# Seven block products for the FFN's first product, the FFN in parts of 8, 8 and 6 tiles, and conditioning vectors in PSUM

## The chip, the cores and the metric

One core of one Trainium2 chip runs the kernel. The metric is the device time of one execution in microseconds; a lower one is better.

## What is computed

One step of a small diffusion backbone of two layers, for 512 latent tokens and 128 context tokens that share the weights. Each layer: a modulated RMSNorm, a projection into three attention branches, their merge, an output projection, a second modulated norm and a SwiGLU FFN. The part that matters here:

```python
def swiglu(h, w_ffn_in, w_ffn_out):
    a, b = jnp.split(h @ w_ffn_in, 2, axis=-1)
    return (jax.nn.silu(a) * b) @ w_ffn_out

def modulation(cvec, w_mod, b_mod):
    m = jax.nn.silu(cvec) @ w_mod + b_mod
    return [t[:, None, :] for t in jnp.split(m, N_MOD, axis=-1)]
...
    x = x + g2 * swiglu(rmsnorm(x, lp['norm2_g']) * (1.0 + sc2) + sh2, lp['w_ffn_in'], lp['w_ffn_out'])
```

The width is 1024, the FFN's inner width 2816, that is 22 tiles of 128; `modulation` is computed for two vectors, that of the request and that of the context. All is float32.

## The kernel before

**Data.** Activations lie transposed: 8 k-tiles of 128 features by 640 tokens, taken in two halves of 320. A float32 product runs as three TensorE passes over split operands: `group` (lines 404 to 414) multiplies high by high, high weight by low input and low weight by high input. Each weight chunk (128 x 1024) is loaded to `raw`, its high part copied by ACT to `whi` (line 311) and its low part, `raw - whi`, made by POOL into `wlo` (line 350). There are two `raw` buffers and four each of `whi` and `wlo`; `weights` (line 357) runs this for all chunks in the order of `plan`.

**FFN.** `ffn_in` takes a part of the inner tiles. A tile has a gate chunk and a value chunk; for each half of the tokens it makes both products over 8 k-tiles into one PSUM tile `S`, then `after` applies silu (ACT, to `s`), multiplies by the value (DVE, `s<-s,S`), and splits the result into high (ACT) and low (DVE, `act<-s,act`). `ffn_out` then multiplies the part's tiles with the second weight and adds the result to the residual `x` (DVE, `x<-S,mo,x`). There were two parts of 11 tiles (`SEG`). `FO_SPLIT` says from which step of the last part the first half of the tokens is finished before the second, so that the norm of the first half can begin.

**Conditioning.** `mod_dve` computes modulation on DVE while other work runs: 512 columns of the transposed weight come to `mr`, and a multiply with a running sum over silu of the vector, `cb` in SBUF (line 515), gives one partial sum. There are 24 sets a layer; 8 are made at the kernel's start in other ways, 12 behind the first attention, the rest in layer 0's FFN.

**Order.** A planner (`_Order`) writes out the order of every engine from estimated costs when the program is built; `DVE`, `ACT`, `POOL` and `SP` then go strictly in that order. Each generator has a priority (lower first: norms 8, weight preparation 20, work behind a product 40, conditioning 200, the dense products 1000), and conditioning fills what is left. Its cost in the plan is `MOD_SPREAD`. `SP` issues all loads.

Of the kernel before, what the change touches and what calls it, by code (L numbers as in the profile page):

```python
# [32 lines left out]
P = 128  # L33
# [37 lines left out]
WO_SPLIT, FO_SPLIT = 4, 66  # L71

SEG = 11
PARTS = [range(a, min(a + SEG, NF)) for a in range(0, NF, SEG)]

# [7 lines left out]
MOD_SOON, MOD_SPREAD = 0.7, 1.4  # L83
# [172 lines left out]
class _Trunk:  # L256
# [41 lines left out]

    def ev(self):
        return _Event()  # L300
# [56 lines left out]
    def weights(self, plan):  # L357

        self.chunks = []
        todo = []  # L360
        for p in plan:
            c = {"src": p, "loaded": self.ev(), "hi_ok": self.ev(), "lo_ok": self.ev()}
            todo.append(c)
        self.chunks = list(todo)

        def load(c):
            c["raw"] = yield from self.get("raw", [P, CH])
            yield self.dma(c["raw"], self.I["w"][c["src"]], 128 * 4 * CH)
            self.o.fire(c["loaded"])

        def hi():
            for c in todo:
                yield self.wait(c["loaded"])
                yield ("acq", "whi")
                yield ("acq", "wlo")
                c["hi"], c["lo"] = self.t("whi", [P, CH], F32R), self.t("wlo", [P, CH], F32R)
                yield self.act(c["hi"], c["raw"], AF.Copy)
                self.o.fire(c["hi_ok"])

        def lo():  # L380
            for c in todo:
                yield self.wait(c["hi_ok"])
                yield self.ptt(c["lo"], c["raw"], c["hi"].bitcast(F32), ALU.subtract)
                self.rel("raw")
                self.o.fire(c["lo_ok"])
# [6 lines left out]
        for g in (load_rest, hi, lo):  # L392
            self.o.spawn(g(), 20)
        return [lambda c=c: load(c) for c in todo[:2]]

    def chunk(self):
        c = self.chunks.pop(0)
        yield self.wait(c["lo_ok"])
        return c["hi"], c["lo"]
# [89 lines left out]
    def mod_dve(self, sets, prio, each):  # L489
# [3 lines left out]
        pieces = [(l, j, q, i, self.ev(), {}) for l, j in sets for q in range(2) for i in range(2)]  # L493

        def load():
            cb = yield from self.get("cb", [P, 2, D])
            yield self.dma(cb, self.I["cb"], 128 * 8 * D)
            yield self.act(cb, cb, AF.Silu)
            self.cb = cb
            self.o.fire(cb_ok)  # L500
            for l, j, q, i, e, d in pieces:
                d["raw"] = yield from self.get("mr", [P, 512])
# [1488 lines left out]
```

## Time and profile before

| | us |
|---|---|
| three runs, median (lowest to highest) | 2482.03 (2476.64 to 2484.36) |
| profiled execution, its own time | 2480.7 |
| its span, first to last instruction | 2478.9 |
| PE busy in the span | 2381.0 |
| DVE, ACT, POOL busy | 1646.1, 1097.4, 907.2 |
| mean granted clock of PE | 0.983 of 2.4 GHz |

A busy share is an average over the whole span. A row of a timeline gives the start in us from the span's beginning, the duration, the engine, the line and the operation, with its output and inputs by the program's tile names; square brackets tell how long the engine had been idle and what ended that.

### The profile page before, as it was taken

The page shows a single profiled execution, that of the slowest core. Times are in us where ns is not written, and L with a number is a line of the kernel's source. Part 1 is how long each engine was busy: PE and PEld are TensorE (multiplying, and loading weights), DVE is VectorE, ACT ScalarE, POOL GpSimd, SP SyncE. Part 2 cuts the span into 40 slices and gives each one's busy share as a digit, 9 for nine tenths or more (in the row PEclk, how much of TensorE's full clock was granted, in tenths as well). Part 3 has the DMA queues.
Part 4 walks back from the last instruction along what each step waited for, and adds up shares of the span by engine and source line. Part 5 has one row for each costly group of instructions (what it writes and reads, how often), then busy time and mean ns, then how long its engine had stood idle before and what let it go on. Part 6 is the DMA issues. An engine that isn't in the chain of part 4 may idle for free.

```text
span 2478.9 us, 44317 instructions
## 1 busy us (share of the span) xinstructions
PE 2381.0 (96%) x17084; PEld 2332.7 (94%) x17084; DVE 1646.1 (66%) x3924; ACT 1097.4 (44%) x2566; POOL 907.2 (37%) x656
## 2 busy tenths in 40 slices
PE   7998889999999999999989998999999999999997
PEld 4998889999988999999989997999999999999997
DVE  7588898678799666676677879887774462212224
ACT  5666566556323322122257664666552342212221
POOL 3534322433433433333345434224333343333331
PEclk9999999999999999999999999999999999999999
DMA  6211111111454444344422111101112322222221
GB/s 235 88 45 57 38 43 35 48 52 44 145 191 141 153 143 150 133 156 139 150 88 70 53 59 43 35 29 63 44 52 73 106 77 77 77 77 71 75 77 60
DMA packets 84739, 216.54 MB, mean 87 GB/s; under 512 B 9648, under 2 KB 23600, under 8 KB 84272
## 3 DMA queue, kind: packets, MB, share of 16 engines
q1 hardware_dynamic: 84528, 213.71, 25.6%
q8 instruction: 135, 2.21, 0.4%
q14 instruction: 76, 0.62, 0.1%
HBM read 206.85 MB, written 6.82 MB: 86 GB/s over the span
## 4 chain that ended last, share of the span: by engine, by line
PE 76%; DVE 18%; issue 2%; ACT 1%; DMA 1%; POOL 0%; SPq 0%; DVEq 0%; ACTq 0%
PE S L411 12%; PE S L410 12%; PE S L412 12%; PE B L410 6%; PE B L412 6%; PE B L411 6%; PE B L1024 3%; PE B L718 3%; PE B L720 3%; PE B L719 3%; PE S L996 2%; PE S L995 2%; DVE nu L338 2%; DVE P L346 2%; PE B L1260 2%
## 5 line engine op out<-in xcount | busy, mean ns | idle before, releaser
L350 POOL TENSOR_TENSOR wlo<-raw,whi 128x1024 fp32r<-128x1024 f32 x268 | 659.6, 2465 | 906.6 <-ACT whi L311 906.2
L411 PE MATMUL S<-h,whi 128*128 128x320 f32 x1408 | 438.7, 312 | 6.5 <-DVE h L338 5.8
L410 PE MATMUL S<-h,whi 128*128 128x320 f32 x1408 | 438.5, 311 | 0.0
L412 PE MATMUL S<-h,wlo 128*128 128x320 f32 x1408 | 437.4, 311 | 0.0
L311 ACT ACTIVATE whi<-raw 128x1024 fp32r<-128x1024 f32 x268 | 282.8, 1056 | 271.7 <-PE S L411 227.2
L718 PE MATMUL B<-whi,h 128*128 128x256 f32 x928 | 278.3, 300 | 1.0 <-DVE u L334 0.5
L411 PEld LDWEIGHTS S<-h,whi 128*128 128x128 f32 x1408 | 266.1, 189 | 9.4 <-DVE h L338 7.0
L720 PE MATMUL B<-whi,h 128*128 128x256 f32 x928 | 266.3, 287 | 3.7 <-DVE h L338 3.1
L410 PEld LDWEIGHTS S<-h,whi 128*128 128x128 f32 x1408 | 266.1, 189 | 0.8 <-ACT h L311 0.4
L412 PEld LDWEIGHTS S<-h,wlo 128*128 128x128 f32 x1408 | 266.3, 189 | 0.0
L719 PE MATMUL B<-wlo,h 128*128 128x256 f32 x928 | 265.7, 286 | 0.0
L515 DVE SCALAR_TENSOR_TENSOR md<-mr,cb 128x512 f32<-128x512 f32 x320 | 260.2, 813 | 5.5 <-DMA mr<-wt 0.8
L410 PE MATMUL B<-h,whi 128*128 128x320 f32 x768 | 245.2, 319 | 1.0 <-ACT th L311 1.0
L412 PE MATMUL B<-h,wlo 128*128 128x320 f32 x768 | 238.5, 311 | 0.0
L411 PE MATMUL B<-h,whi 128*128 128x320 f32 x768 | 238.2, 310 | 0.0
L334 DVE TENSOR_TENSOR s<-s,S 128x320 f32<-128x320 f32 x88 | 42.9, 488 | 281.2 <-ACT s L311 281.2
L311 ACT ACTIVATE P<-S,mx 128x768 f32<-128x768 f32 (+4 forms) x240 | 180.6, 754 | 88.3 <-DVE mx L1009 68.8
L410 PE MATMUL S<-act,whi 128*128 128x320 f32 x704 | 218.2, 310 | 0.0
L411 PE MATMUL S<-act,whi 128*128 128x320 f32 x704 | 217.8, 309 | 0.0
L412 PE MATMUL S<-act,wlo 128*128 128x320 f32 x704 | 217.7, 309 | 0.0
L410 PE MATMUL B<-u,whi 128*128 128x320 f32 x640 | 203.3, 318 | 5.2 <-ACT u L311 4.0
L411 PE MATMUL B<-u,whi 128*128 128x320 f32 x640 | 199.4, 312 | 0.8 <-DVE u L334 0.7
(162 smaller groups left out, 5918.3 us busy)
## 6 DMA issues: line engine op xcount, KB each, us to landing
raw<-w SPq DMA_DIRECT2D x268, 512.0 KB, 3.3
mr<-wt SPq DMA_DIRECT2D x160, 256.0 KB, 3.0
mraw<-wm SPq DMA_DIRECT2D x24, 256.0 KB, 4.8
x<-x SPq DMA_DIRECT2D x8, 320.0 KB, 5.6
xr<-x SPq DMA_DIRECT2D x16, 160.0 KB, 3.2
xm<-x SPq DMA_DIRECT2D x8, 320.0 KB, 4.3
xr<-xm SPq DMA_DIRECT2D x16, 160.0 KB, 2.6
y<-h SPq DMA_DIRECT2D x16, 160.0 KB, 1.8
```

Source lines behind the costliest of these rows:

```text
L311: fn = lambda: self.nc.scalar.activation(out, in_, func, **kw)
L338: _n(out), lambda: self.nc.vector.scalar_tensor_tensor(out, a, s, b, op0=op0, op1=op1),
L346: _n(out), lambda: self.nc.vector.tensor_scalar(out, a, s1, s2, op0=op0, **kw), not _in_psum(a), cols
L350: return ("POOL", 0.147 + 0.0021 * _n(out), lambda: self.nc.gpsimd.tensor_tensor(out, a, b, op=op), 0.08)
L410: mm(out, lhsT=wh, rhs=xh, start=first, stop=False)
L411: mm(out, lhsT=wh, rhs=xl, start=False, stop=False)
L412: mm(out, lhsT=wl, rhs=xh, start=False, stop=last)
L515: yield ("DVE", each, lambda w=d["raw"], b=b, r=r: nc.vector.scalar_tensor_tensor(md, w, 1.0, b, op0=ALU.mult, op1=ALU.mult, accum_out=r), ...
L718: mm(d, lhsT=hh, rhs=wh, start=kt == 0, stop=False)
L719: mm(d, lhsT=hh, rhs=wl, start=False, stop=False)
L720: mm(d, lhsT=hl, rhs=wh, start=False, stop=kt == KT - 1)
L1024: nc.tensor.transpose(t[:, i * P:(i + 1) * P], a, self.ident)
```

## The change

Inner tiles 0 to 2 (`PLAIN`) stay as they were; tiles 3 to 21 go through `seven`. There gate and value, the two halves of k and the two halves of the tokens make a 2 x 2 by 2 x 2 block product, done in Winograd's form of Strassen's scheme: seven products of 4 k-tiles instead of eight, and sums before and after. `seven_inputs` makes the sums of `h` once a layer (DVE), with their splits, into eight buffers `ht`. `sums` makes four weight sums of 512 columns for every tile (DVE) into `ws` and over `raw2`, a second raw buffer for the value chunk. Four splits follow where there were two, one of them of half width. `post` combines the products with seven additions that read PSUM (DVE) and one copy (ACT).

The FFN now holds six PSUM banks one by one (`open_banks`) and the hidden product stays in PSUM: `hidden` multiplies there, and the split reads it from there. The other two banks hold silu of the two conditioning vectors, half of their 1024 columns at a time, reloaded between passes (`vectors`, with `home` "T"; in layer 0's earlier place both halves are in "S"). So each multiply of the conditioning reads one input from PSUM. The sets 20 to 23 of a layer are made in its own FFN, the next layer's 0 to 19 in layer 0's. The FFN has parts of 8, 8 and 6 tiles, and the planner counts 0.75 instead of 1.4 for a conditioning step.

```diff
-WO_SPLIT, FO_SPLIT = 4, 66
-SEG = 11
+WO_SPLIT, FO_SPLIT = 4, 6
+SEG = 8
 PARTS = [range(a, min(a + SEG, NF)) for a in range(0, NF, SEG)]
+PLAIN = 3
...
+    def open_banks(self):
+        self.banks = []
+        for _ in range(2):
+            t = yield from self.get("S", [P, 1024])
+            self.banks += [t[:, 0:HALF], t[:, 512:512 + HALF]]
+        for _ in range(2):
+            self.banks.append((yield from self.get("D", [P, 512]))[:, 0:HALF])
+        self.o.pool("Z", len(self.banks))
...
+            if c["seven"]:
+                yield self.wait(self.f_ok[c["l"]])
+                c["raw2"] = yield from self.get("raw2", [P, CH])
+                yield self.dma(c["raw2"], I["w"][c["l"], c["src"][1]], 128 * 4 * CH)
+                self.o.fire(c["loaded2"])
+        def sums():
+            for c in todo:
+                if not c["seven"]:
+                    continue
+                yield self.wait(c["loaded2"])
+                ws = c["ws"] = yield from self.get("ws", [P, CH])
+                ra, rb = c["raw"], c["raw2"]
+                yield self.tt(ws[:, h1], rb[:, h1], rb[:, h2], ALU.add)
+                yield self.tt(ws[:, h2], ws[:, h1], ra[:, h1], ALU.subtract)
+                self.o.fire(c["s1"])
+                yield self.tt(rb[:, h1], ra[:, h1], rb[:, h1], ALU.subtract)
+                self.o.fire(c["s3"])
+                yield self.wait(c["lo_ok"][1])
+                yield self.tt(ws[:, h2], ra[:, h2], ws[:, h2], ALU.subtract)
+                self.rel("raw")
+                self.o.fire(c["s4"])
...
+                for n, e in enumerate(("loaded", "s1", "s4", "s3") if c["seven"] else ("loaded",)):
+                    yield ("acq", "whi")
+                    yield ("acq", "wlo")
+                    c["hi"].append(self.t("whi", [P, CH], F32R))
+                    c["lo"].append(self.t("wlo", [P, CH], F32R))
+                    yield self.wait(c[e])
+                    x, w = self.part(c, n)
+                    yield self.act(c["hi"][n][:, 0:w], x, AF.Copy)
+                    self.o.fire(c["hi_ok"][n])
...
+                for n, done in enumerate((None, None, "ws", "raw2") if c["seven"] else ("raw",)):
+                    yield self.wait(c["hi_ok"][n])
+                    x, w = self.part(c, n)
+                    yield self.ptt(c["lo"][n][:, 0:w], x, c["hi"][n][:, 0:w].bitcast(F32), ALU.subtract)
+                    if done:
+                        self.rel(done)
+                    self.o.fire(c["lo_ok"][n])
...
+        def vectors():
+            for _ in range(2):
+                cv.append((yield from self.get(home, [P, n])))
+            used = None
+            for at, _, ok, done in plan:
+                if used is not None:
+                    yield self.wait(used)
+                for c in range(2):
+                    for i in range(2) if at is None else (at,):
+                        r = yield from self.get("cr", [P, 512])
+                        yield self.dma(r, self.I["cb"][:, c, i * 512:(i + 1) * 512], 128 * 4 * 512)
+                        to = 0 if at is not None else i * 512
+                        yield self.act(cv[c][:, to:to + 512], r, AF.Silu)
+                        self.rel("cr")
+                self.o.fire(ok)
+                used = done
...
+        plain = [f for f in part if f < PLAIN]
+        steps = [(f, half) for g in (plain[:2], plain[2:]) for half in range(2) for f in g]
...
+        for f in part:
+            if f >= PLAIN:
+                act[f] = yield from self.get("act", [P, 2, 2, HALF], F32R)
+                yield from self.seven(h, act[f], act_ok[f])
...
+            t = (yield from self.get("act", [P, 2, 2, HALF], F32R)).rearrange("p a b t -> p a (b t)").bitcast(F32)
+            x, y = t[:, 0], t[:, 1]
+            for kt, z in ((k, x), (k2, y)):
+                yield self.tt(z, h[kt][:, 0].bitcast(F32), h[kt][:, 1].bitcast(F32), ALU.add)
+            yield self.tt(x[:, a], x[:, b], x[:, a], ALU.subtract)
+            yield self.tt(x[:, b], y[:, b], x[:, b], ALU.subtract)
+            yield self.tt(y[:, b], y[:, b], x[:, a], ALU.subtract)
+            yield self.tt(y[:, a], y[:, a], y[:, b], ALU.subtract)
...
+            def split(z, e, k=k, hits=hits):
+                d = self.ht[k][e] = (yield from self.get("ht", [P, 2 * T], F32R)).rearrange("p (e t) -> p e t", e=2)
+                yield self.act(d[:, 0], z, AF.Copy)
+                yield self.tt(d[:, 1], z, d[:, 0].bitcast(F32), ALU.subtract)
+                hits()
...
+        def post():
+            s_ok = [self.ev(), self.ev()]
+            yield self.wait(done[1])
+            v = yield from self.get("fv", [P, HALF])
+            yield self.act(v, p[1], AF.Copy)
+            self.bank_done(p[1])
+            yield self.wait(done[6])
+            u = yield from self.get("fu", [P, HALF])
+            yield add(u, p[6], v)
+            self.bank_done(p[6])
+            yield self.wait(done[2])
+            yield add(p[2], p[2], v)
+            o.spawn(gate(0, p[2], s_ok[0]), 39)
+            yield self.wait(done[5])
+            yield add(v, p[5], u)
+            yield self.wait(done[7])
+            yield add(u, p[7], u)
+            self.bank_done(p[7])
+            yield add(p[5], p[5], u)
+            yield self.wait(done[3])
+            yield add(p[3], p[3], v)
+            self.rel("fv")
+            o.spawn(gate(1, p[3], s_ok[1]), 39)
+            def second():
+                yield self.wait(s_ok[1])
+                yield from self.hidden(silu[1], p[5], act[:, :, 1], hit)
+            o.spawn(second(), 40)
+            yield self.wait(done[4])
+            yield add(p[4], p[4], u)
+            self.rel("fu")
+            yield self.wait(s_ok[0])
+            yield from self.hidden(silu[0], p[4], act[:, :, 0], hit)
...
+        def go(i, part, col, xs):
+            p[i] = yield from self.bank()
+            yield self.wait(c["lo_ok"][part])
+            for k in range(n):
+                wh, wl = (t[part][:, col + k * P:col + (k + 1) * P] for t in (c["hi"], c["lo"]))
+                xh, xl = xs(k)
+                yield self.group(p[i], wh, wl, xh, xl, k == 0, k == n - 1)
+            o.fire(done[i])
+        yield from go(1, 0, 0, lambda k: two(h[k], a))
+        for ok in self.ht_ok:
+            yield self.wait(ok)
+        yield from go(6, 1, half, lambda k: two(self.ht[k][1], b))
+        yield from go(2, 0, half, lambda k: two(h[n + k], a))
+        self.chunk_done()
+        yield from go(5, 1, 0, lambda k: two(self.ht[k][0], a))
+        self.chunk_done()
+        yield from go(7, 3, 0, lambda k: two(self.ht[k][0], b))
+        yield from go(3, 2, 0, lambda k: two(h[n + k], b))
+        self.chunk_done()
+        yield from go(4, 3, half, lambda k: two(self.ht[k][1], a))
...
+    def hidden(self, s, d, out, hit):
+        yield self.tt(d, d, s, ALU.mult)
+        self.rel("s")
+        yield self.act(out[:, 0], d, AF.Copy)
+        yield self.tt(out[:, 1], d, out[:, 0].bitcast(F32), ALU.subtract)
+        self.bank_done(d)
+        hit()
...
-        split = FO_SPLIT if end else KT * n
+        split = (FO_SPLIT if end else KT) * n
...
-            fctx = self.pool("f", {"act": SEG, "s": 1})
+            fctx = self.pool("f", {"act": SEG, "s": 2, "ht": 8, "raw2": 2, "ws": 1, "fu": 1, "fv": 1})
             o.fire(f_open)
+            o.fire(self.f_ok[l])
+            o.spawn(self.seven_inputs(*h2), 12)
...
+            here, ahead = [(l, j) for j in range(20, 24)], [(l + 1, j) for j in range(20)]
+            steps = [((0,), here), ((1,), here)]
             if not last:
-                mctx = self.pool("m", dict(mods, mr=8))
-                here = [(l, j) for j in range(20, 24)] if l == 0 else []
-                self.mod_dve(here + [(l + 1, j) for j in range(24)], 200, MOD_SPREAD)
+                steps += [((1,), ahead), ((0,), ahead)]
+            self.mod_dve(steps, 200, MOD_SPREAD, "T")
```

The planner moves much, so here is what stands in the order of three places. First DVE between two products of layer 0's FFN: before, with `s` and `act` the plain tile's hidden value and `md` the conditioning;

```order
L515 SCALAR_TENSOR_TENSOR md_10658,ma_11022<-mr_10808,cb_10583 128x512
L334 TENSOR_TENSOR s_11058<-s_11058,S_10986 128x320
L515 SCALAR_TENSOR_TENSOR md_10658,ma_11022<-mr_10808,cb_10583 128x512
L334 TENSOR_TENSOR act_10985<-s_11058,act_10985 128x320
L515 SCALAR_TENSOR_TENSOR md_10658,ma_11022<-mr_10818,cb_10583 128x512 x2
L515 SCALAR_TENSOR_TENSOR md_10658,ma_11022<-mr_10851,cb_10583 128x512 x2
L334 TENSOR_TENSOR s_11120<-s_11120,S_11059 128x320
```

and now, in a seven-product tile of the second part, from the third weight sum (over `raw`) to the fourth; the two that make `ws` stand four and two rows ahead of it, with the low part of a hidden half behind each.

```order
L362 TENSOR_TENSOR raw_2176_12485<-raw_12445,raw_2176_12485 128x512
L362 TENSOR_TENSOR fu_12632<-B_10374,fv_12607 128x320
L616 SCALAR_TENSOR_TENSOR md_10583,ma_10584<-mr_12483,B_10579 128x512
L362 TENSOR_TENSOR S_10373<-S_10373,fv_12607 128x320
L616 SCALAR_TENSOR_TENSOR md_10583,ma_10584<-mr_12483,B_10580 128x512
L362 TENSOR_TENSOR fv_12607<-B_10375,fu_12632 128x320
L616 SCALAR_TENSOR_TENSOR md_10583,ma_10584<-mr_12548,B_10579 128x512
L362 TENSOR_TENSOR fu_12632<-S_10373,fu_12632 128x320
L616 SCALAR_TENSOR_TENSOR md_10583,ma_10584<-mr_12548,B_10580 128x512
L362 TENSOR_TENSOR B_10375<-B_10375,fu_12632 128x320
L616 SCALAR_TENSOR_TENSOR md_10583,ma_10584<-mr_12572,B_10579 128x512
L362 TENSOR_TENSOR ws_12611<-raw_12445,ws_12611 128x512
```

The hidden product's SBUF inputs are gone, the sums of `fu` and `fv` with PSUM have come in, and five conditioning steps with `B` (the vectors' banks) lie between weight sums. Second, POOL in the FFN of layer 0, before;

```order
L350 TENSOR_TENSOR wlo_10698<-raw_10644,whi_10697 128x1024
L350 TENSOR_TENSOR wlo_10715<-raw_10670,whi_10714 128x1024
L350 TENSOR_TENSOR wlo_10844<-raw_10727,whi_10843 128x1024
L350 TENSOR_TENSOR wlo_10854<-raw_10764,whi_10853 128x1024
L350 TENSOR_TENSOR wlo_10984<-raw_10866,whi_10983 128x1024
```

and now for one tile and the first split of the next: the middle two read `ws`, one of half width.

```order
L378 TENSOR_TENSOR wlo_11091<-raw_10848,whi_11090 128x1024
L378 TENSOR_TENSOR wlo_11112<-ws_11048,whi_11111 128x1024
L378 TENSOR_TENSOR wlo_11151<-ws_11048,whi_11150 128x512
L378 TENSOR_TENSOR wlo_11183<-raw_1993_10923,whi_11182 128x1024
L378 TENSOR_TENSOR wlo_11235<-raw_11028,whi_11234 128x1024
```

POOL has four operations in place of two for a tile, and two read what DVE's sums write. Third, DVE where layer 0's FFN begins, `h` being the second norm's result: before;

```order
L338 SCALAR_TENSOR_TENSOR h_10201<-nu_10523,mo_84,h_10201 128x128
L338 SCALAR_TENSOR_TENSOR h_10202<-nu_10539,mo_84,h_10202 128x192
L338 SCALAR_TENSOR_TENSOR h_10202<-nu_10539,mo_84,h_10202 128x128
L334 TENSOR_TENSOR s_10565<-s_10565,S_10450 128x320
L334 TENSOR_TENSOR act_10449<-s_10565,act_10449 128x320
L334 TENSOR_TENSOR s_10623<-s_10623,S_10536 128x320
L334 TENSOR_TENSOR act_10364<-s_10623,act_10364 128x320
L334 TENSOR_TENSOR s_10696<-s_10696,S_10626 128x320
L515 SCALAR_TENSOR_TENSOR md_10658,ma_10659<-mr_10660,cb_10583 128x512
L334 TENSOR_TENSOR act_10449<-s_10696,act_10449 128x320
```

and now, from the third k-tile's sums (tile `act` serves as scratch) on.

```order
L362 TENSOR_TENSOR act_10718<-h_10189 128x640
L362 TENSOR_TENSOR ht_10716<-act_10638,ht_10716 128x640
L362 TENSOR_TENSOR act_10718<-h_10193 128x640
L362 TENSOR_TENSOR ht_10717<-act_10638,ht_10717 128x640
L362 TENSOR_TENSOR act_10718<-act_10718 128x320
L362 TENSOR_TENSOR ws_10725<-raw_1963_10703 128x512
L362 TENSOR_TENSOR act_10718<-act_10718 128x320
L362 TENSOR_TENSOR ws_10725<-ws_10725,raw_10675 128x512
L362 TENSOR_TENSOR act_10718<-act_10718 128x320
L362 TENSOR_TENSOR raw_1963_10703<-raw_10675,raw_1963_10703 128x512
L362 TENSOR_TENSOR act_10718<-act_10718 128x320
L362 TENSOR_TENSOR S_10373<-S_10373,s_10736 128x320
```

The additions of `h`, the low parts of `ht` and the first tile's weight sums have come between the norm and the hidden values of the plain tiles.

## Rows read from the trace of the kernel before

**Rows 1.** The page: busy time of each engine, and the chain by engine.

```profile
PE 2381.0 (96%) x17084; PEld 2332.7 (94%) x17084; DVE 1646.1 (66%) x3924; ACT 1097.4 (44%) x2566; POOL 907.2 (37%) x656
...
PE 76%; DVE 18%; issue 2%; ACT 1%; DMA 1%; POOL 0%; SPq 0%; DVEq 0%; ACTq 0%
```

**Rows 2.** Busy time by stretch: from:to, length, busy (instructions) by engine, granted clock, DMA.

```profile
785.00:801.30 16.30, 12.65 (x52) 10.43 (x52) 15.54 (x26) 8.21 (x16) 7.91 (x5) 0.69 0.38 133
801.30:947.00 145.70, 145.70 (x995) 145.70 (x995) 97.67 (x217) 46.76 (x82) 52.88 (x24) 1.00 0.44 149
...
2160.00:2300.00 140.00, 140.00 (x956) 140.00 (x955) 25.70 (x42) 28.35 (x38) 46.70 (x20) 1.00 0.21 73
```

**Rows 3.** Timeline of PE in layer 0's FFN: start, duration, line, operation.

```profile
820.40 0.31 PE L410 MATMUL S<-h,whi 128*128 128x320 f32 x1
...
821.28 0.31 PE L410 MATMUL S<-h,whi 128*128 128x320 f32 x1
```

**Rows 4.** Costliest groups, by form: count, busy, mean ns, idle before them.

```profile
L350 POOL TENSOR_TENSOR wlo<-raw,whi 128x1024 fp32r<-128x1024 f32 x268 | 659.6, 2465 | 906.6 <-ACT whi L311 906.2 <-POOL kac L350 0.3
...
L311 ACT ACTIVATE whi<-raw 128x1024 fp32r<-128x1024 f32 x268 | 282.8, 1056 | 271.7 <-PE S L411 227.2 <-issue 16.5 <-PE B L411 14.3
...
L334 DVE TENSOR_TENSOR act<-s,act 128x320 fp32r<-128x320 f32 x88 | 130.6, 1484 | 33.9 <-ACT act L311 33.8
...
L334 DVE TENSOR_TENSOR s<-s,S 128x320 f32<-128x320 f32 x88 | 42.9, 488 | 281.2 <-ACT s L311 281.2
```

**Rows 5.** Timeline of DVE in layer 0's FFN, with POOL idle.

```profile
831.69 0.69 DVE L515 SCALAR_TENSOR_TENSOR md<-mr,cb 128x512 f32<-128x512 f32 x1
832.31 0.08 DVE L515 DVE_READ_ACCUMULATOR md<-mr,cb 128x1 f32 x1
832.42 0.69 DVE L515 SCALAR_TENSOR_TENSOR md<-mr,cb 128x512 f32<-128x512 f32 x1
...
833.04 0.48 DVE L334 TENSOR_TENSOR s<-s,S 128x320 f32<-128x320 f32 x1
833.44 0.68 DVE L515 SCALAR_TENSOR_TENSOR md<-mr,cb 128x512 f32<-128x512 f32 x1
```

**Rows 6.** Timelines of POOL and of DVE at two places of layer 0's FFN.

```profile
840.10 2.44 POOL L350 TENSOR_TENSOR wlo<-raw,whi 128x1024 fp32r<-128x1024 f32 x1 [1.20 <-ACT whi L311]
...
840.41 2.48 DVE L334 TENSOR_TENSOR act<-s,act 128x320 fp32r<-128x320 f32 x1
...
1008.64 2.41 POOL L350 TENSOR_TENSOR wlo<-raw,whi 128x1024 fp32r<-128x1024 f32 x1 [4.22 <-ACT whi L311]
...
1009.36 1.14 DVE L338 SCALAR_TENSOR_TENSOR x<-S,mo,x 128x320 f32<-128x320 f32 x3 [2.45 <-PE S L412]
```

**Rows 7.** Timelines of PE, DVE, POOL and ACT behind layer 0's second norm.

```profile
792.81 0.64 PE L411 MATMUL S<-h,whi 128*128 128x320 f32 x1 [2.89 <-DVE h L338]
793.24 0.47 PE L412 MATMUL S<-h,wlo 128*128 128x320 f32 x1
793.51 0.47 PE L410 MATMUL S<-h,whi 128*128 128x320 f32 x1
...
808.82 1.82 DVE L338 SCALAR_TENSOR_TENSOR h<-nu,mo,h 128x192 fp32r<-128x192 f32 x4
...
815.04 2.41 POOL L350 TENSOR_TENSOR wlo<-raw,whi 128x1024 fp32r<-128x1024 f32 x1 [5.14 <-ACT whi L311]
...
826.07 5.03 POOL L350 TENSOR_TENSOR wlo<-raw,whi 128x1024 fp32r<-128x1024 f32 x2 [4.63 <-ACT whi L311]
...
838.64 0.44 ACT L311 ACTIVATE s<-S 128x320 f32<-128x320 f32 x1 [2.56 <-PE S L412]
```

**Rows 8.** Timelines of DVE and PE at the end of layer 0's FFN.

```profile
1251.36 0.55 DVE L338 SCALAR_TENSOR_TENSOR x<-S,mo,x 128x320 f32<-128x320 f32 x1 [2.19 <-PE S L412]
...
1264.45 0.38 PE L720 MATMUL B<-whi,h 128*128 128x256 f32 x1 [2.46 <-DVE h L338]
...
1270.35 0.90 PE L614 MATMUL B<-ssq,ones 128*128 128x320 f32 x1 [2.84 <-DVE ssq L334]
```

More of the change, by code (lines that the diff above doesn't have):

```diff
@@ L390, in load_rest, with part @@
                 yield from load(c)
-        for g in (load_rest, hi, lo):
+        for g in (load_rest, sums, hi, lo):
             self.o.spawn(g(), 20)
         return [lambda c=c: load(c) for c in todo[:2]]
+    def part(self, c, n):
+        if not c["seven"] or n == 0:
+            return c["raw"], CH
+        return (c["ws"], CH) if n == 1 else (c["ws"][:, CH // 2:CH], CH // 2) if n == 2 else (c["raw2"], CH)
     def chunk(self):
         c = self.chunks.pop(0)
-        yield self.wait(c["lo_ok"])
-        return c["hi"], c["lo"]
+        yield self.wait(c["lo_ok"][0])
+        return c["hi"][0], c["lo"][0]
     def chunk_done(self):
@@ new lines, in seven, with gate @@
+    def seven(self, h, act, act_ok):
+        o = self.o
+        c = self.chunks.pop(0)
+        n = KT // 2
+        a, b = slice(0, HALF), slice(HALF, T)
+        p = {}
+        done = {i: self.ev() for i in range(1, 8)}
+        hit = self.counter(2, lambda: o.fire(act_ok))
+        add = lambda d, x, y: self.tt(d, x, y, ALU.add)
+        silu = {}
+        def gate(half, d, ok):
+            s = yield from self.get("s", [P, HALF])
+            yield self.act(s, d, AF.Silu)
+            self.bank_done(d)
+            silu[half] = s
+            o.fire(ok)
+        def post():
[30 more added lines that the diff above has]
+            yield from self.hidden(silu[0], p[4], act[:, :, 0], hit)
+        o.spawn(post(), 40)
+        def go(i, part, col, xs):
[6 more added lines that the diff above has]
+            o.fire(done[i])
+        two = lambda t, s: (t[:, 0, s], t[:, 1, s])
+        half = CH // 2
+        yield from go(1, 0, 0, lambda k: two(h[k], a))
+        for ok in self.ht_ok:
+            yield self.wait(ok)
+        yield from go(6, 1, half, lambda k: two(self.ht[k][1], b))
[7 more added lines that the diff above has]
+        yield from go(4, 3, half, lambda k: two(self.ht[k][1], a))
+        self.chunk_done()
@@ L1542, in ffn_out @@
             if j == n - 1:
-                self.o.spawn(after(m, half, d, free[m]), 7)
+                self.o.spawn(after(m, half, d), 7)
     def open_x(self, sq=1):
@@ L1626, in dense @@
             yield self.wait(f_open)
+            yield from self.open_banks()
             for part in PARTS:
@@ L1770, in plan @@
             for part in PARTS:
-                out += [(l, O_FI + 2 * f + e) for f in part for e in range(2)]
+                for f in part:
+                    two = [O_FI + 2 * f + e for e in range(2)]
+                    out += [(l, t) for t in two] if f < PLAIN else [(l, tuple(two))]
                 n = len(part) * KT // 8
```

167 lines of the change are left out of this document (99 added, 68 removed).

## The prediction

> **What bounds the kernel now.** I read the page's first and fourth parts, then busy time by stretch, then single instructions. The page shows TensorE busy for 96% of the span and with 76% of the chain that ended last [rows 1]. The stretches show that the FFN is stricter still: between 801.3 and 947 us, and between 2160 and 2300 us, PE has no idle time at all at a granted clock of 1.00, while DVE is busy 97.7 of 145.7 us in layer 0 and 25.7 of 140.0 us in layer 1, and POOL about a third in both [rows 2]. So inside the FFN a matmul that is taken out is worth its full issue interval, as long as what feeds PE stays covered. That interval is in the timeline of PE: the matmul at 820.40 and the one six later at 821.28 are 0.88 us apart, 0.1467 us each [rows 3]; the 0.31 us that a row shows overlaps its neighbours.
>
> **What goes.** A plain FFN tile is 2 x 8 x 2 x 3 = 96 matmuls (gate and value, 8 k-tiles, two halves of tokens, three passes), a seven-product tile 7 x 4 x 3 = 84. Nineteen tiles in each of two layers lose 12: 456 matmuls, which is also the difference of 16706 and 16250 rows on PE. At 0.1467 us that is 66.9 us [rows 3]. A seven-product tile then takes PE 84 x 0.1467 = 12.3 us where a plain one took 14.1. The Trainium skill (TensorE: Matmul & The Clock Gate, "Wait — 56ns, not 53.3ns?") gives N / 2.4 GHz plus 2.5 ns between two warm matmuls, which for 320 columns is an estimate of 135.8 ns; by it the term would be 61.9 us. The row was measured in this very loop, so 66.9 stands.
>
> **What has to hide behind it.** Prices first. A DVE tensor_tensor of 320 columns that is not held up has its successor 0.40 us later, a multiply-reduce of 512 columns for the conditioning 0.73 us later, of which 0.62 us come before its read-out row [rows 5]; I take 0.62 for the 512-column weight sums and, in proportion, 0.77 for 640 columns (bounds 0.40 and 0.80, twice the row of 320). A split costs ACT 1.06 us and, alone on its port, POOL 2.41 us [rows 4, 6]. A seven-product tile needs 3.5 splits (POOL 8.4 us; ACT 3.7, and five short operations like silu's 0.44 [rows 7], 5.9 in all) and on DVE 4 sums and 11 operations with a PSUM input: 4 x 0.62 + 11 x 0.40 = 6.9 us. Each engine alone fits into 12.3 us.
>
> The trouble is that DVE and POOL don't work alone. At 840.41 a DVE tensor_tensor with both inputs in SBUF took 2.48 us, ending as POOL's operation of 840.10 ended; the same form takes 0.49 otherwise, and its mean is 1484 ns. A DVE operation on PSUM ran at 1009.36 in the middle of POOL's from 1008.64 and took 1.14 us for three, 0.38 each [rows 4, 6]. The change moves the FFN's own two forms and the conditioning into the second kind, which frees DVE, and adds four sums of the first kind to each tile. The Trainium skill (SBUF — State Buffer, "Who interferes with whom") has the rule behind it: two SBUF inputs contend with a GpSimd operation that reads SBUF, and whichever starts first keeps the port for all of it. It speaks against the four sums; what it costs at worst is the rival below.
>
> **Where it costs in a tile.** Take t = 0 at the tile's first matmul; a product takes 12 x 0.1467 = 1.76 us. The four weight buffers come free after products 3, 4, 6 and 7: 5.3, 7.0, 10.6 and 12.3 us. POOL then splits part 0 of the next tile until 8.9, part 1 until 11.3; DVE's last sum needs that, POOL's part 2 ends at 13.9, its part 3 at 16.4. DVE's first sum for the tile after needs part 2's end, by when POOL has taken part 3: it waits 2.4 us, until 4.1 in the next tile. DVE goes in order, so all behind it waits too: the second half of the hidden tile, the second product's sum. Six accumulators give this room. What decides is the loop from first sum to last sum and back. From a tile's first weight sum to its last (the listing shows most of it) stand 3 sums, 7 PSUM operations and, in layer 0, five multiply-reduces: 1.9 + 2.8 + 3.7 = 8.3 us with rounding, so the last sum begins at 12.4 where part 1 was done at 11.4. That makes layer 0's tiles late by 1.0 us each; part 3 is wanted by the fifth product at 7.0, so the first 2.9 us are free. In layer 1's later tiles the five are missing, 4.7 us replace 8.3, and nothing is late. Layer 0's second part has about five dense tiles (1 to 2 us lost), its third part four, each with one or two tiny SBUF additions that finish a conditioning set and can stand behind POOL; at 2.4 us for the worse of them, some 2.5 us late a tile, 10 less 2.9. I take 8 us for layer 0 and 0 for layer 1 (bounds 0, and 30 and 5 if every tile were late by 1.5).
>
> **Where it costs at the FFN's start.** The sums of h for the right side are new: 8 additions of 640, 16 of 320, 8 low parts of 640 columns. The last h is written at 810.64 now [rows 7]. Behind it DVE has, up to the wait for the third tile's first half, 13 operations of 640 (10.0 us), 14 of 320 that each read what the one before wrote (the whole 0.49 of a row each, 6.9), 6 of PSUM (2.4), 4 sums and 2 multiply-reduces (3.9): 23.2 us, to 834, and POOL has four splits in this time (the first and the last two are shown) [rows 7], each good for up to 2.4 us of DVE. Then follow another 5 us. Product two of the first seven-product tile wants them at 838.6 (the third tile's end, which silu's row gives) plus 1.76 = 840.3 [rows 7]. So they come between 839 and 848: 0 to 8 us of idle PE. A wait of this size has a tail: after PE's 2.89 us at 792.81 the next matmuls stand 0.27 us apart, and the stretch from 785 to 801.3 has a granted clock of 0.69, that is, part of it at 1.2 GHz [rows 2, 7]. I take 7 us for each layer, tail included: 14 (bounds 0 and 24).
>
> **The seams.** At the FFN's end the second half of the last two row blocks covers the norm of the first half. It was 22 groups of 0.44 us, 9.7 us; with six tiles in the last part it is 12, 5.3 us. From the first half's last residual (1251.36) to the matmul that follows the first h (1264.45) are 13.1 us, and PE waited 2.46 us of them [rows 8]. Less cover by 4.4 us costs up to 4.4 more, but the second half's sum of squares is then early, on which PE waited 2.84 us at 1270.35 [rows 8]: I take 3 (bounds 0 and 4.4), and 1 for the same shift at the very end (0 to 3). One part more means 16 more residuals a layer, each with six accumulators to wait in and 7.0 us of matmuls beside 0.8 us of DVE: nothing. The second weight buffer's loads, the conditioning's reload in halves and SP's queue cost nothing as long as loads take some 3 us of a 12.3 us tile; if that goes, the first sums are late as above. No saving is booked for DVE's freed waits: nothing in the FFN waited for them.
>
> **Sum.** -66.9 + 8 + 14 + 3 + 1 = -41 us on the profiled execution's 2480.7 us, which lies 1.3 us under the median of the runs, 2482.0. From that median: **2441 us**.
>
> **Rivals.** (1) The cover holds: starts, queue and seams together cost under 12 us. For it: DVE idles between halves at the start now, and layer 1's last sum is ready at 8.8 where it is let go at 11.4. 2415 to 2427; 25%. (2) Layer 0's queue costs much more, 25 to 30 us instead of 8, since the conditioning fills every gap of DVE and a late DVE holds accumulators as well: 2455 to 2470; 17%. Against it: lateness also lets POOL's part 3 end before DVE asks. (3) Slower. Each of the four sums stands behind a whole POOL operation in all 38 tiles: 4 x 2.41 = 9.6 us on top of 6.9 is 16.5 us of DVE against 12.3 us of PE, 4.2 us x 38 = 160 us, less 66.9, plus 18 for starts and seams: 2593. It turns the sign once a tile loses (66.9 - 18) / 38 = 1.3 us. For it: the mean of 1484 ns against 488 for the PSUM form [rows 4]. Against it: POOL has only four operations a tile, and three sums come when it waits for buffers. 5%. (4) That the matmuls don't fall away can be left out; the rows of PE are counted. My own case, 2428 to 2455, has 50%, and 3% remain for no difference.
>
> **Range and chances.** 2416 to 2468 takes in my case, nearly all of (1) and most of (2). A difference of 0.3%, 7.4 us, is about what a measurement of this kernel can tell from none. Faster 92%, the same 3%, slower 5%.
>
> **What would show it.** Right: PE's matmuls still 0.1467 us apart in the FFN; one wait of some 5 us for ht at the first seven-product tile of each layer; short waits of PE for wlo in layer 0's second and third part and none in layer 1's; the low parts of act near 490 ns. Wrong: waits for wlo in every tile of layer 1 (then the loop is longer than worked out), PE waiting for accumulators, or matmuls further apart.

## The result: slower by 2.4%, and the profile after

The changed kernel took 2540.9 us (median of four runs, 2536.5 to 2544.1) where the kernel before took 2482.8 beside it: a ratio of 1.024 [1.022, 1.026]. I had said 2441, within 2416 to 2468, and gave "slower" 5%, for another reason than the one that came true. The profiled execution has a span of 2541.8 us; the kernel before has 2478.9.

The page of the changed kernel, the rows that answer to [rows 1]:

```profile
PE 2360.0 (93%) x16628; PEld 2281.8 (90%) x16628; DVE 1885.4 (74%) x4454; ACT 1184.6 (47%) x2708; POOL 1038.5 (41%) x732
...
PE 70%; DVE 24%; issue 3%; ACT 2%; POOL 1%; DMA 0%; SPq 0%; DVEq 0%; ACTq 0%; POOLq 0%
```

The 456 matmuls are gone (17084 to 16628). TensorE's share of the chain has fallen from 76 to 70%, and VectorE's has risen from 18 to 24: the chain now runs through VectorE more often. To see where, I cut both spans at the same four events, the product that sums the second half's squares (on the tile of ones) at each norm behind the first. The timelines of PE in the two kernels, before and after (for layer 0's end, 1270.35 us before, see [rows 8]):

```profile
795.25 1.40 PE L614 MATMUL B<-ssq,ones 128*128 128x320 f32 x2 [0.40 <-DVE ssq L334]
...
1998.69 0.87 PE L614 MATMUL B<-ssq,ones 128*128 128x320 f32 x1 [0.41 <-DVE ssq L334]
...
2466.81 1.29 PE L614 MATMUL B<-ssq,ones 128*128 128x320 f32 x2 [2.72 <-DVE ssq L334]
```

```profile
789.18 1.41 PE L716 MATMUL B<-ssq,ones 128*128 128x320 f32 x2 [8.89 <-DVE ssq L362]
...
1301.89 1.43 PE L716 MATMUL B<-ssq,ones 128*128 128x320 f32 x2 [4.80 <-DVE ssq L362]
...
2036.38 0.87 PE L716 MATMUL B<-ssq,ones 128*128 128x320 f32 x1 [0.40 <-DVE ssq L362]
...
2529.62 0.81 PE L716 MATMUL B<-ssq,ones 128*128 128x320 f32 x2 [3.52 <-DVE ssq L362]
```

The differences are the stages: layer 0's FFN 475.1 to 512.7 us, layer 1's attention 728.3 to 734.5, layer 1's FFN 468.1 to 493.2. Each FFN should have lost 33.5 us (half of 66.9) and has gained 37.6 and 25.1. Layer 1's gain is the telling one, since I had booked nothing there behind the start. Two stretches by engine, in layer 0's first part, where PE is busy for 63.3 of 74 us, and in the middle of layer 1's FFN (columns as in [rows 2]):

```profile
842.00:916.00 74.00, 63.32 (x394) 60.11 (x392) 62.99 (x127) 25.97 (x42) 39.50 (x19) 0.95 0.34 118
...
2190.00:2300.00 110.00, 100.07 (x648) 96.26 (x647) 61.55 (x98) 33.02 (x52) 54.21 (x25) 0.98 0.19 68
```

In the second, 648 matmuls ran where 110 / 0.1467 = 750 fit, with VectorE idle for 44% of the time and GpSimd for half of it. No engine is full there, and PE still waits. What for is told by the groups of PE by tile (busy, mean ns | idle just before them, releasers). An S is a tile of two banks, a B one of one bank; the FFN's two accumulators from pool `D` appear as B:

```profile
L485 PE MATMUL B<-h,whi 128*128 128x320 f32 x956 | 302.8, 317 | 0.0
...
L485 PE MATMUL S<-act,whi 128*128 128x320 f32 x484 | 153.0, 316 | 10.4 <-DVE x L366 7.3 <-DVE S L362 1.7 <-DVE act L362 0.9
L485 PE MATMUL S<-h,whi 128*128 128x320 f32 x460 | 151.8, 330 | 34.0 <-DVE S L362 14.8 <-DVE fu L362 7.2 <-ACT s L339 5.2
...
L485 PE MATMUL S<-ht,whi 128*128 128x320 f32 x376 | 123.2, 328 | 40.2 <-DVE S L362 12.3 <-ACT s L339 7.4 <-DVE act L362 5.1
...
L485 PE MATMUL B<-ht,whi 128*128 128x320 f32 x232 | 73.8, 318 | 0.0
...
L485 PE MATMUL B<-act,whi 128*128 128x320 f32 x220 | 68.2, 310 | 0.0
```

The products of h, ht and act lose 34.0 + 40.2 + 10.4 = 84.6 us when their accumulator is an S, and nothing when it is a B (the group of h on B also holds products outside the FFN). One such wait, in the timelines of PE and DVE in layer 1:

```profile
2247.88 0.31 PE L487 MATMUL S<-ht,wlo 128*128 128x320 f32 x1
...
2248.76 0.31 PE L487 MATMUL S<-h,wlo 128*128 128x320 f32 x1
2249.66 0.41 PE L485 MATMUL S<-h,whi 128*128 128x320 f32 x1 [0.59 <-DVE S L362]
2249.91 0.30 PE L486 MATMUL S<-h,whi 128*128 128x320 f32 x1
2250.05 0.31 PE L487 MATMUL S<-h,wlo 128*128 128x320 f32 x1
2250.95 0.41 PE L485 MATMUL S<-h,whi 128*128 128x320 f32 x1 [0.59 <-DVE S L362]
```

```profile
2249.10 0.50 DVE L362 TENSOR_TENSOR S<-S,fu 128x320 f32<-128x320 f32 x1 [1.14 <-PE S L487]
2250.40 0.50 DVE L362 TENSOR_TENSOR S<-S,s 128x320 f32<-128x320 f32 x1 [0.79 <-PE S L487]
```

The rows from 2248.76 on are groups of three matmuls (one k-tile each) of one product, which is already under way in its accumulator, and between its groups PE waits for VectorE's operation on an S, twice; VectorE in turn had waited 1.14 and 0.79 us for PE's matmul into an S. Nothing in the arithmetic joins them: the sum S<-S,fu belongs to a finished product. What joins them is `open_banks`: it takes two tiles S of 1024 columns and makes two accumulators of each, columns 0 to 319 and 512 to 831. Theory A was therefore: the program guards a tile as a whole, so each use of one half waits for what runs on the other (called the tie below). Theory B, from my own rivals: VectorE is late through the port and the conditioning, and S merely shows it.

### The profile page after: what moved, and what is told of

It is laid out like the page before. It is cut to its first block, busy times and chain, and to the rows that moved or that the text cites. A ratio compares the mean times of both kernels' runs of the same rounds, so it can differ in the third digit from the quotient of the medians.

```text
span 2541.8 us, 44487 instructions
## 1 busy us (share of the span) xinstructions
PE 2360.0 (93%) x16628; PEld 2281.8 (90%) x16628; DVE 1885.4 (74%) x4454; ACT 1184.6 (47%) x2708; POOL 1038.5 (41%) x732
## 4 chain that ended last, share of the span: by engine, by line
PE 70%; DVE 24%; issue 3%; ACT 2%; POOL 1%; DMA 0%; SPq 0%; DVEq 0%; ACTq 0%; POOLq 0%
PE B L485 10%; PE B L486 9%; PE B L487 9%; PE S L485 7%; PE S L487 6%; PE S L486 6%; PE B L1126 3%; PE B L820 3%; PE B L822 3%; PE B L821 3%; PE S L1098 2%; PE S L1097 2%; PE B L1362 2%; DVE act L362 2%; PE B L1361 2%
## 5 line engine op out<-in xcount | busy, mean ns | idle before, releaser
L485 PE MATMUL B<-h,whi 128*128 128x320 f32 x956 | 302.8, 317 | 0.0
L486 PE MATMUL B<-h,whi 128*128 128x320 f32 x956 | 296.3, 310 | 0.0
L378 POOL TENSOR_TENSOR wlo<-ws,whi 128x1024 fp32r<-128x1024 f32 x76 | 140.9, 1854 | 166.1 <-ACT whi L339 147.4
L487 PE MATMUL B<-u,wlo 128*128 128x320 f32 x640 | 198.4, 310 | 0.0
L1111 DVE TENSOR_REDUCE mx<-S 128x1 f32<-128x768 f32 (+4 forms) x240 | 181.6, 763 | 11.6 <-PE S L1098 8.9
L820 PEld LDWEIGHTS B<-whi,h 128*128 128x128 f32 x928 | 182.4, 197 | 4.2 <-ACT nat L339 1.5
L362 DVE TENSOR_TENSOR PT<-B,PT 128x512 fp32r<-128x512 f32 (+2 forms) x264 | 155.7, 608 | 39.6 <-ACT PT L339 36.9
L822 PEld LDWEIGHTS B<-whi,h 128*128 128x128 f32 x928 | 181.8, 196 | 2.5 <-POOL h L378 2.2
L485 PE MATMUL S<-h,whi 128*128 128x320 f32 x460 | 151.8, 330 | 34.0 <-DVE S L362 14.8
L821 PEld LDWEIGHTS B<-wlo,h 128*128 128x128 f32 x928 | 182.7, 197 | 0.2 <-issue 0.2
L485 PEld LDWEIGHTS B<-h,whi 128*128 128x128 f32 x956 | 180.9, 189 | 0.0
L486 PEld LDWEIGHTS B<-h,whi 128*128 128x128 f32 x956 | 180.8, 189 | 0.1
L487 PEld LDWEIGHTS B<-h,wlo 128*128 128x128 f32 x956 | 180.4, 189 | 0.0
```

The lines of the kernel that those rows point to most:

```text
L362: return self.dve(_n(out), lambda: self.nc.vector.tensor_tensor(out, a, b, op=op))
L378: return ("POOL", 0.147 + 0.0021 * _n(out), lambda: self.nc.gpsimd.tensor_tensor(out, a, b, op=op), 0.08)
L485: mm(out, lhsT=wh, rhs=xh, start=first, stop=False)
L486: mm(out, lhsT=wh, rhs=xl, start=False, stop=False)
L487: mm(out, lhsT=wl, rhs=xh, start=False, stop=last)
L820: mm(d, lhsT=hh, rhs=wh, start=kt == 0, stop=False)
```

## The experiments

Times are medians; the kernel before took 2479.8 to 2483.2 beside them.

**Own tiles, and the conditioning less dense.** Four runs. The first takes the four accumulators from a pool of their own; PE, VectorE, ScalarE and GpSimd keep their order. (The 499 us that the expectations give for layer 1's FFN are 493.2 between the marks used here.)

```diff
-            t = yield from self.get("S", [P, 1024])
-            self.banks += [t[:, 0:HALF], t[:, 512:512 + HALF]]
...
+        self.sctx.close()
+        self.qctx = self.pool("q", {"Q": 4}, space=PSUM)
+        for _ in range(4):
+            self.banks.append((yield from self.get("Q", [P, 512]))[:, 0:HALF])
```

> The changed kernel, but the four accumulators that were halves of two two-bank tiles S are four tiles of one bank each; the order on VectorE, ScalarE and GpSimd is the same. Theory A (a matmul into one half of S waits for what VectorE and ScalarE still do with the other half, and the reverse): the waits of PE on S go, the groups on S and on B show the same mean idle, and 80 to 100 us of the 2541 come back: 2440 to 2460, layer 1's FFN about 445 us instead of 499. Theory B (VectorE is late through the port it shares with GpSimd, and through the conditioning placed too densely): VectorE is as late as before, the waits only move to other accumulators: within 10 us of 2541.

Measured: 2463.1 us, 0.9925 [0.991, 0.994] of the kernel before; span 2456.5, that is 85.3 us less than the changed kernel's 2541.8 (77.8 by the medians), where the waits on S made 84.6. Layer 0's FFN fell from 512.7 to 469.6 us, layer 1's from 493.2 to 450.3. The groups of PE and the middle of layer 1's FFN in this run:

```profile
L492 PE MATMUL B<-h,whi 128*128 128x320 f32 x956 | 303.6, 318 | 2.1 <-DVE act L369 2.1
...
L492 PE MATMUL Q<-act,whi 128*128 128x320 f32 x484 | 150.4, 311 | 4.0 <-ACT act L346 4.0
...
L492 PE MATMUL Q<-h,whi 128*128 128x320 f32 x460 | 146.2, 318 | 0.0
...
L492 PE MATMUL Q<-ht,whi 128*128 128x320 f32 x376 | 117.2, 312 | 3.7 <-ACT ht L346 1.7 <-ACT s L346 1.3 <-ACT fv L346 0.4
```

```profile
2148.00:2258.00 110.00, 110.00 (x752) 110.00 (x751) 70.77 (x118) 42.20 (x68) 67.17 (x32) 1.00 0.21 71
```

The same three groups lose 7.7 us now, and PE is gapless where it lost a seventh. Theory A holds, in place and nearly in size: 2463.1 is 3 us over its range of 2440 to 2460, and layer 1's FFN 5 us over the 445.

```diff
-MOD_SOON, MOD_SPREAD = 0.7, 0.75
+MOD_SOON, MOD_SPREAD = 0.7, 1.4
```

> The changed kernel, with layer 0's share of the next layer's conditioning set less densely on VectorE (its spread constant 1.4 instead of 0.75). Theory A: the waits on S stay, layer 1's FFN is the same 499 us; at most 15 us less in all. Theory B: layer 0's FFN loses about 30 us, 2505 to 2515, and layer 1's FFN stays.

> Four accumulators in tiles of their own and the conditioning less dense, both. Theory A: within 10 us of the run with own tiles alone, 2435 to 2460. Theory B: as the run with the conditioning spread alone, 2505 to 2515.

Measured: 2562.4 us with shared tiles, 2481.0 with own tiles. Both theories missed the cost: with 1.4 the conditioning does not end before the FFN does, and the next layer's norm stands still for it. The timeline of PE with own tiles:

```profile
1301.21 0.58 PE L827 MATMUL B<-whi,h 128*128 128x256 f32 x1 [41.07 <-DVE md L623]
```

Apart from that the runs say two things. Own tiles are worth the same with either density (2562.4 - 2481.0 = 81 us, against 2540.9 - 2463.1 = 78). And with own tiles the thinner conditioning made layer 0's FFN 453.4 us instead of 469.6: density matters there, for 16 us (16 with shared tiles too, 512.7 to 496.5). Neither theory had layer 1's FFN move, but with shared tiles it fell from 493.2 to 483.8 and with own tiles from 450.3 to 444.4: the spread constant also sets how densely the sets 20 to 23 of layer 1 lie in its own FFN, so these edits thin both layers.

```diff
-                yield self.tt(ws[:, h1], rb[:, h1], rb[:, h2], ALU.add)
-                yield self.tt(ws[:, h2], ws[:, h1], ra[:, h1], ALU.subtract)
...
-                yield self.tt(rb[:, h1], ra[:, h1], rb[:, h1], ALU.subtract)
...
-                yield self.tt(ws[:, h2], ra[:, h2], ws[:, h2], ALU.subtract)
```

> Four accumulators in tiles of their own, and the four sums of the weights left out: the parts hi and lo are cut from the loaded weights themselves, so the FFN's first product is taken with other weights. It prices the sums and their standing at the port. Theory A: 5 to 15 us less than with own tiles alone, nearly all in layer 0. Theory B: 40 us or more less than that, in both layers.

Measured: 2428.4 us, 35 under own tiles alone; layer 0's FFN 448.6 (21 less), layer 1's 442.8 (7 less). That is more than A's 5 to 15 and less than B's 40: the sums, with the splits' waiting for them, are a cost of their own beside the tiles, most of it in layer 0.

**Number or sharing?** Only one half of each S is used, so that four accumulators are left, none of them shared.

```diff
-            self.banks += [t[:, 0:HALF], t[:, 512:512 + HALF]]
+            self.banks.append(t[:, 0:HALF])
```

> The changed kernel with only four accumulators: one half of each S tile and the two tiles of one bank; the other half of each S stays unused, so that no tile is shared. Theory A (the shared tile costs, not the number): faster than the changed kernel's 2541 with two accumulators fewer, 2475 to 2520. Rival (the FFN needs the number, and six tied ones are still better than four free ones): slower than 2541.

Measured: 2470.0 us, 0.9955 [0.994, 0.997], better even than A's 2475. Four accumulators on their own beat six of which four are tied in pairs by 71 us. The two more are worth 7 us (2463.1).

**What is left in layer 0.** Own tiles throughout. Density in smaller steps, and the chain of the sums made shorter:

```diff
-MOD_SOON, MOD_SPREAD = 0.7, 0.75
+MOD_SOON, MOD_SPREAD = 0.7, 0.85
```

> Six accumulators in tiles of their own, and layer 0's conditioning a little less dense (0.85 instead of 0.75; 1.4 left 45 products behind the FFN's end and a wait of 41 us). If density on VectorE is what remains in layer 0: its FFN 460 us or less instead of 469.6, no wait for the conditioning, 2450 to 2458. If the chain of the sums sets the pace there: within 4 us of 2463.

```diff
-                yield self.wait(c["lo_ok"][1])
-                yield self.tt(ws[:, h2], ra[:, h2], ws[:, h2], ALU.subtract)
-                self.rel("raw")
+                yield self.wait(c["lo_ok"][0])
+                yield self.tt(ra[:, h1], ra[:, h2], ws[:, h2], ALU.subtract)
+                c["ws_done"]()
```

> Six accumulators in tiles of their own; the last of the four sums goes into the loaded weights' own first half instead of back into ws, so ws is free after its first low part, not after the third, and the conditioning is as dense as in the changed kernel. If the chain through ws (sum, high part, low part, sum, high part, low part, 16 us a tile in layer 0's middle against 12.3 us of matmuls) sets the pace: layer 0's FFN 450 to 456 us instead of 469.6, waits for low parts gone, 2443 to 2452. If density on VectorE does: within 4 us of 2463.

> Own tiles, the last sum into the loaded weights, and the conditioning at 0.85. If the chain through ws is the limit: within 4 us of the run with 0.75 and the same sums. If both count: 2440 to 2447.

Measured: 2449.7, 2471.6 and 2463.4 us. The shorter chain is slower by 8 and by 14 us, in both FFNs (478.4 and 460.6 with 0.75): this is outside the ranges of both cases. Shortening my loop through ws brought no gain, so nothing here shows it to be the limit. The edit also holds the loaded weights until the third low part, so the next load starts later; whether that is its cost was not tried. The density of 0.85 gave its 13 us, but not where I had expected: layer 0's FFN stayed at 469.1, and layer 1's, which the same constant thins, fell from 450.3 to 444.1; another 3.7 us lie ahead of layer 0's FFN, where the code is the same.

```diff
-MOD_SOON, MOD_SPREAD = 0.7, 0.75
+MOD_SOON, MOD_SPREAD = 0.7, 0.92
```

> Six accumulators in tiles of their own, the conditioning at 0.92 instead of 0.85 (2450) or 0.75 (2463). If less density helps as long as the products end before layer 0's FFN does: 2440 to 2448. If 0.85 had already all of it: within 4 us of 2450. No wait for the conditioning longer than 2 us in either case.

```diff
-                            md, w, 1.0, b, op0=ALU.mult, op1=ALU.mult, accum_out=r), 0.13)
+                            md[:, 0:16], w[:, 0:16], 1.0, b[:, 0:16], op0=ALU.mult, op1=ALU.mult, accum_out=r), 0.13)
```

> Own tiles at 0.75, the same order on every engine, but each product of the conditioning takes 16 of its 512 columns (the rest of each sum is left out, so layer 0's later modulations and layer 1's are other numbers). It takes some 0.5 us from each of 192 instructions on VectorE in layer 0's FFN. If VectorE's fullness there is what remains of layer 0's 28 us over the 441.6: its FFN 445 to 452 us instead of 469.6. If the port alone is (the sums stretched beside GpSimd): 465 or more.

```diff
-                yield self.tt(ws[:, h1], rb[:, h1], rb[:, h2], ALU.add)
-                yield self.tt(ws[:, h2], ws[:, h1], ra[:, h1], ALU.subtract)
+                yield self.slow(1.7, self.tt(ws[:, h1], rb[:, h1], rb[:, h2], ALU.add))
+                yield self.slow(1.4, self.tt(ws[:, h2], ws[:, h1], ra[:, h1], ALU.subtract))
```

> Own tiles at 0.75; the planner that sets the order is told 1.7 and 1.4 us for the first two of the four sums, near what they last beside GpSimd, instead of 0.6. If the order is set too tight because those are priced too low: layer 0's FFN 455 to 462 us, 2442 to 2455. If the order does not matter there: within 4 us of 2463.

Measured: 2432.4 (0.9806 [0.979, 0.982]), 2428.9 and 2438.9 us. The first and the third are faster than either of their cases had it, by 8 and 3 us; the second's FFN (447.8) is where fullness had it. The same 171 us of layer 0's middle, by engine, with own tiles at 0.75, at 0.92, and at 0.75 with short conditioning:

```profile
905.00:1076.00 171.00, 161.48 (x1078) 157.89 (x1076) 162.82 (x360) 56.11 (x87) 90.06 (x41) 1.00 0.47 157
```

```profile
905.00:1076.00 171.00, 171.00 (x1168) 171.00 (x1167) 139.65 (x336) 56.55 (x85) 93.39 (x43) 1.00 0.48 160
```

```profile
905.00:1076.00 171.00, 171.00 (x1168) 171.00 (x1167) 119.57 (x396) 56.83 (x85) 95.51 (x44) 1.00 0.53 174
```

At 0.75 VectorE is full (162.8 of 171) and PE loses 90 matmuls; with the third run's instructions in the very same order, only the conditioning's shorter, nothing is lost. In the same stretch VectorE is busy for 153.3 us at 0.85, where PE runs 1121 matmuls, and for 142.4 us with the sums' true costs, where it runs 1168. Layer 0's FFN goes from 469.6 to 453.2 and 447.8. So what is left there is how full VectorE is in such a stretch. Sums and conditioning both add to it, and leaving out either takes back some 21 us. The amount of work alone does not decide: telling the planner what the sums last leaves all of it in and does nearly as much (454.5). The gain is not smooth in the density: for the whole of layer 0's FFN 0.85 gave nothing, and 0.92 sixteen. The order that the planner finds jumps, and I have no account of which rows make the jump.

**The seam.**

```diff
-WO_SPLIT, FO_SPLIT = 4, 6
+WO_SPLIT, FO_SPLIT = 4, 4
```

> Own tiles, conditioning at 0.92, and the last part of the FFN's second product turns to one half after the other from output tile 4 instead of 6: four tiles of 18 matmuls, 10.6 us, stand between the end of the first half and the end of the second, where there are 5.3 us now and were 9.7 us in the kernel before. If the short cover is what the seam costs: the wait of 4.8 us for ssq at layer 0's end and that of 3.5 at layer 1's fall to about 2.8 each, layer 1's attention from 736 back to 729, 2421 to 2427. If the seam's cost has another cause: within 3 us of 2432.

Measured: 2433.4 us, no change. The wait for ssq at layer 0's end fell from 4.80 to 3.47 us, but layer 0's FFN and layer 1's attention together took 1192.3 instead of 1189.3. So the second case holds: the short cover is not the seam's cost.

## Why the prediction was wrong

**The step that failed** is the sentence "Six accumulators give this room". I counted accumulators and took them for interchangeable. Four of them were halves of two tiles, and a tile is guarded as a whole: a matmul into one half waits for VectorE's or ScalarE's operation on the other, and the reverse. That cost 85.3 us of span (own tiles against shared ones; 77.8 by the medians), more than the 66.9 that the change was to bring, and alone turns the sign. It stood in the diff, and the text named "PE waiting for accumulators" as a sign of being wrong, but no rival and no term carried it. The Trainium skill (PSUM — Partial Sum Buffer, "PSUM bank collisions raise a hardware error") asks for guards by bank and quadrant, not by address; by it the two halves of a tile of 1024 columns, which lie in two banks of 2 KiB, need no guard against each other. The run with own tiles agrees: with one bank to a tile the waits are gone, and the engines' orders are the same.

The other steps, with the tie taken away:

- **Matmuls, -66.9.** Right. The page counts 456 fewer (the 16706 and 16250 that I gave are another count with the same difference), they still take 0.88 us for six (from 2247.88 to 2248.76 us in the timeline above), and 752 ran in the gapless 110 us. Layer 1's FFN at 0.92 comes near the sum: 468.1 - 33.5 = 434.6, measured 442.2.
- **FFN's start, 7 a layer.** Right in size for layer 1, too high for layer 0. With own tiles at the change's density PE waits for ht 1.66 and 2.38 us in layer 1, and the granted clock is 0.50 from 2043.1 to 2049.8 us; half of these 6.7 us is an estimated 3.4 lost, 7.4 with the waits. In layer 0 it waits 2.28 us, with 0.50 from 838.2 to 841.4 us, an estimated 3.9 in all. At 0.92 layer 0's waits are 1.12 and 0.53 us without a fall of the clock. Layer 1's are the two below, with 0.50 from 2019.3 to 2026.1 us: about 7.2 of the 7.6 us by which 442.2 is over 434.6.

```profile
2019.41 0.63 PE L492 MATMUL Q<-ht,whi 128*128 128x320 f32 x1 [2.86 <-ACT ht L346]
2020.94 0.63 PE L493 MATMUL Q<-ht,whi 128*128 128x320 f32 x1 [0.89 <-DVE ht L369]
```

- **Layer 0's queue, 8.** Too low. With own tiles at the change's density short conditioning takes back 21.8 us (469.6 against 447.8), and some 8 in layer 1, where I had 0 (450.3 against 442.6). Some 4 of the first and most of the second are the starts above: with short conditioning PE waits for ht 0.63 and 0.78 us in layer 1 and not at all in layer 0. I had priced the four sums at 0.62 us each, 2.5 a tile. In the changed kernel they took, by the groups of DVE:

```profile
L362 DVE TENSOR_TENSOR ws<-raw 128x512 f32<-128x512 f32 x38 | 64.7, 1702 | 1.9 <-POOL wlo L378 1.5
...
L362 DVE TENSOR_TENSOR ws<-ws,raw 128x512 f32<-128x512 f32 x38 | 34.0, 895 | 0.1
L362 DVE TENSOR_TENSOR raw<-raw,raw 128x512 f32<-128x512 f32 x38 | 31.7, 833 | 0.0
...
L362 DVE TENSOR_TENSOR ws<-raw,ws 128x512 f32<-128x512 f32 x38 | 26.0, 684 | 5.7 <-POOL wlo L378 5.6
...
L362 DVE TENSOR_TENSOR act<-S,act 128x320 fp32r<-128x320 f32 x52 | 25.1, 483 | 11.8 <-PE S L487 8.2 <-ACT act L339 2.1 <-ACT fv L339 1.2
```

  That is 4.1 us a tile (4.9 with own tiles), 1.6 (2.4) over my price, where rival (3) had 9.6 over it. PE's waits for wlo came as foreseen, 15.2 us in 12 of them with own tiles, nearly all in layer 0. The first sum stands behind GpSimd most often, as I had worked out for the sum behind part 2: 23 of the 38 took over 1 us, and each of these began during a split of GpSimd and ended some 0.55 us after it, while an unhindered one took 0.68; the last row shows the other side: the low parts of act, 1484 ns before [rows 4], fell to 483 as foreseen, since one input is in PSUM. The Trainium skill (SBUF — State Buffer, "Who interferes with whom") has both as one rule, and these rows agree with it. Rival (2), 25 to 30 us, was the better guess at this term, and its 2455 to 2470 takes in the 2463.1 of own tiles.
- **Seams, 3 and 1.** The second is nothing behind the last mark (12.1 us in both kernels); just ahead of it PE's wait for ssq grew from 2.72 to 3.52 us. The first is near its size, but not by my argument. At layer 0's end PE waited 2.46, 0.59, 2.84 and 0.62 us before, and 4.80, 0.74, 0.87 and 0.84 us at 0.92, which is 0.7 more in all. The granted clock is 0.50 from 1234.3 to 1247.8 us at 0.92, and was from 1265.6 to 1275.6 us before; at half the clock the 3.5 us more are an estimated 1.8 lost. That makes 2.5 us (about 4 with short conditioning, where the clock is 0.50 from 1233.4 to 1250.3 us). The cover of 5.3 us that I argued with is not the reason, as the last run shows.
- **What is over beside these.** With short conditioning layer 0's FFN and layer 1's attention together are 1184.6 us, 14.6 over 1203.4 - 33.5. PE's remaining waits for wlo in layer 0 are 6.3 of them, which brings layer 0's queue without its start to some 24; the seam is about 4, and 12 matmuls that stood ahead of the first mark before and stand behind it now are 1.8. The other 2 to 3 us are open.
- **Ahead of the FFN**, a stage that I had at nothing: 795.3 us before, 781.8 to 789.2 in the runs of this family. Of this 1.8 us are the same 12 matmuls. It is shorter although PE now waits 8.89 us for ssq at its end (marks above), where it had waited 2.26, 0.35, 2.89 and 0.40 us. It differs by 7 us between kernels whose code is the same there, and was not followed further.

Put together, in us of span: -66.9 (matmuls) + 85.3 (tie) + 21.8 and 7.7 (what short conditioning takes back in the two FFNs) + 7.9 (over in layer 1's FFN) + 14.6 (over in layer 0's FFN and layer 1's attention) - 7.4 (ahead of the FFN, own tiles) = +63.0, against 2541.8 - 2478.9 = +62.9. This closes by construction, since the last three are what is left in each stage, and so it tests nothing. The tie and the two terms of the conditioning are each measured between two runs whose engines keep one order.

Without the tie and with the conditioning thinned to 0.92 the kernel takes 2432 us, faster than the kernel before by 1.9% and than the change as made by 4.3%. That this lies within my range of 2416 to 2468 is partly luck. The stages that I had priced are 40 us of span shorter there, where I had said 41. But the two starts cost some 9 us instead of 14, and costs that I had not named made up for it; and another 13.4 us come from ahead of the FFN, where I had nothing. It is also another density than that of the kernel I forecast.

## What to carry to other kernels

Before you count buffers, ask in what unit the program guards them: two accumulators in one tile are one accumulator with two users, and four separate ones beat six that are tied. A wait in the middle of a product, on a tile that this very product owns, can be the sign of it in a profile, as it was here; compare the idle column of groups that differ in the tile alone. And where an engine fills its gaps with work that has a deadline, test the density in both directions: too dense, here, cost 16 us in one FFN, and too thin kept the next stage waiting for 41 us.

## What was not expected of the hardware

A stall of 5 us at the seam goes with a lower clock for longer than I had seen it before. PE waits 4.80 us for ssq at layer 0's end, and some waits of about 1 us follow; in the next 52 us it is busy for 49.5, and the granted clock is 0.88 (own tiles, density 0.92). In the kernel before, where the wait was 2.84 us, the same 52 us have 0.95:

```profile
1234.99:1286.99 52.00, 49.54 (x354) 47.84 (x355) 31.99 (x80) 31.98 (x88) 30.82 (x36) 0.88 0.24 73
```

```profile
1270.35:1322.35 52.00, 51.38 (x395) 50.76 (x396) 33.29 (x83) 33.61 (x94) 32.25 (x37) 0.95 0.24 78
```

Part of both stretches therefore ran at 1.2 GHz instead of 2.4. Stretches with waits on shared tiles show the same on a small scale: 0.95 and 0.98 in the two of the changed kernel above. Waiting alone does not decide it: of the four stretches shown of FFNs with own tiles, all at 1.00, the one of layer 0 at 0.75 has PE idle for 9.5 of 171 us.
